# A decoder layer with 32 experts: another list of tasks for the first stage, and earlier loads for the second expert

## The chip, the cores and the metric

The kernel runs on one core of a Trainium2 chip. The metric is the device time of one execution in microseconds; lower is better. A core has TensorE (matmuls, with its weight loads counted apart), VectorE, ScalarE, GpSimd, and the queues that issue transfers: SyncE's (SPq), ScalarE's (ACTq) and GpSimd's (POOLq). All of these share 16 transfer engines. The profile calls the engines PE, PEld, DVE, ACT, POOL and SP.

## The reference

One decoder layer on 512 tokens of width 1024, all in float32. The heart of it:

```python
mod = (silu(c) @ w_ada + b_ada); shift1, scale1, gate1, shift2, scale2, gate2 = split(mod, 6)
h = rmsnorm(x, norm1_w) * (1 + scale1) + shift1
proj = h @ w_in                      # DeltaNet q, k, v, z, a, b and attention q, k, v
o_dn = gated_delta_rule(conv_silu(q), conv_silu(k), conv_silu(v))   # 4 heads of 128, chunks of 64
o_sw = sliding_window_attention(q, k, v, sinks)                     # 8 heads of 64, 2 key heads, window 128
x = x + gate1 * (concat(o_dn, o_sw) @ w_out)
h = rmsnorm(x, norm2_w) * (1 + scale2) + shift2
top_val, top_idx = top_k(h @ w_router + b_router, 4)                # of 32 experts
x = x + gate2 * sum over chosen experts of gate * (swiglu(h @ w_up[e] + b_up[e]) @ w_down[e] + b_down[e])
```

The weights of an expert are 8 MB (up) and 4 MB (down); all 32 experts are used, so 384 MB are read.

## The kernel before, in words

**First stage.** Everything up to the choice of experts. The input is scaled, modulated and projected; the DeltaNet part is prepared for two pairs of heads (`p` = 0, 1): projections and convolutions (`project`, `conv`), lengths, decays, and the inverse of a triangular matrix per chunk (`inverse`, L976 ff.), whose steps go to and fro between TensorE, ScalarE and VectorE. The attention heads (`swa_*`) run beside it. Then `recur` steps through 8 chunks, one after the other; `output` turns each into a part of `oT`. Then for each of the four tiles of 128 tokens (`i` = 0 to 3): `out_swa` and `out_delta` (the output projection, L1142 and L1161, 32 matmuls a tile), `out_end` (adds it to the input), `second_norm`, `route` (router, top 4, slot numbers, and a table that gives each expert's tokens), `finish` (adds the gated bias of the down projection and stores the tile). `ranks` counts the tokens of each expert and orders the experts by count; its result `eri` (L1524) says which expert has which rank. `places` turns table and ranking into `gi`, the rows to gather (L1537), and into `si` and `sg`, the rows to add to and their gates.

**The order of the first stage** is written out by a small planner, `Flow`, while the program is built. Each task is a generator that yields (engine, price in us, buffers wanted) ahead of each step. The planner keeps a clock per engine, takes among the tasks whose next step can start first (within `SLACK`) the one of the lowest priority number (`PR`), and so fixes the order of instructions on each engine. On the chip the engines keep to this order and wait for one another by semaphores. A price that is off therefore costs no time by itself; it puts an instruction at the wrong place in its queue.

**Second stage.** The experts run in a fixed order of ranks (`ORDER`). For each, GpSimd clears a tile and gathers the tokens (`gather`, L1697 and L1698), TensorE transposes them (`turn`), multiplies with the up weights (`up_pass`, L1760), the swiglu runs on VectorE and ScalarE, and TensorE multiplies with the down weights (`down`, L1797); GpSimd adds the rows into the output (`put`). Weights come in pieces of 1 MB through 16 slots, in the order up of expert 0, down 0, up 1, up 2, down 1, up 3, ...; a piece waits until TensorE has used the one that held its slot. The first in the order is always expert 0, so its 12 pieces are issued (`ahead`) before the choice is known. Which expert is second comes from `eri`: GpSimd copies the number to `second` behind the first gather, and SyncE's queue reads it there (`fetch_up(1)`, L1882). Four slots are free for it then (`LATE`); the fifth piece waits for the first step of `up_pass` of expert 0. `load_bias` puts an expert's `b_up` into one of two buffers, `spread_bias` copies it over the rows.

The projections of `project` are done as three single-pass matmuls on high and low parts (`mm3`, L317); most other matmuls are plain float32.

## Time and profile before

| | us |
|---|---|
| median of 3 runs | 1483.18 (1478.5 to 1484.42) |
| the profiled execution | 1480.72 |
| its span, first to last instruction | 1478.9 |
| mean granted clock of TensorE | 0.974 |
| busy: PE, DVE, POOL, ACT | 1381.5, 563.8, 261.1, 237.8 |

A busy TensorE is not TensorE at its peak: the ends of matmuls are modelled and overlap. The rows further down are copied from the trace. A row of a timeline begins with start and length; `x8` counts instructions in one merged row; the bracket behind it tells how long the engine stood idle before and what released it. A row of waits reads: who waited, for whom, us in total, times, longest. Clock 1.00 is 2.4 GHz, 0.50 is 1.2 GHz.

### The profile page before, as it was taken

Reading aid. Unit: us, or ns where it says so; the run is one execution under the profiler, and the core shown is the slowest. Engines: PE = TensorE matmul, PEld = TensorE weight load, DVE = VectorE, ACT = ScalarE, POOL = GpSimd, SP = SyncE. Lnnn points to the kernel's source line nnn. Section 1 sums busy time; section 2 is a strip of 40 time slices with the busy share of each in tenths; the row PEclk is TensorE's granted clock in tenths of the full one; section 3 lists DMA queues with packets and bytes.
Section 4 is the critical chain, followed back from the end, with each engine's and each line's share of the span. In section 5 each row is a group of like instructions: output and inputs, shape, how many; then the busy total and the mean of one; then the engine's idle time right before and its main releaser. Section 6 shows DMA issues by size and latency. Waiting matters only on the chain. (4 is left out here: it accounts for less than half of the span.)

```text
span 1478.9 us, 22303 instructions
## 1 busy us (share of the span) xinstructions
PE 1381.5 (93%) x8586; PEld 601.3 (41%) x8586; DVE 563.8 (38%) x1247; ACT 237.8 (16%) x542; POOL 261.1 (18%) x216
## 2 busy tenths in 40 slices
PE   4999999999879999979999999999999999999974
PEld 3766666765443333322333333333333333343311
DVE  6965567566853222212221231223321323232310
ACT  4354354442211000000000000000000000010000
POOL 2213133202331111101011101102110112211110
PEclk9999999999969999999999999999999999999976
DMA  9655300256349999999999999999998999999995
GB/s 302 212 200 204 113 29 30 58 214 277 116 152 407 409 387 402 396 391 412 411 412 400 379 419 394 384 409 393 410 367 349 403 348 404 393 418 415 414 415 229
DMA packets 104980, 476.16 MB, mean 322 GB/s; under 512 B 13992, under 2 KB 39556, under 8 KB 55714
## 3 DMA queue, kind: packets, MB, share of 16 engines
q1 hardware_dynamic: 91842, 453.16, 77.4%
q0 software_dynamic: 11952, 18.75, 5.5%
q10 hardware_dynamic: 1072, 2.70, 0.5%
q8 instruction: 75, 1.23, 0.3%
q14 instruction: 39, 0.32, 0.1%
HBM read 464.14 MB, written 17.22 MB: 325 GB/s over the span
## 5 line engine op out<-in xcount | busy, mean ns | idle before, releaser
L1760 PE MATMUL ps_up<-we,xTe 128*64 128x512 f32 (+1 forms) x3040 | 622.2, 607 | 21.2 <-DMA we<-in_w_up_dram 16.8
L1760 PEld LDWEIGHTS ps_up<-we,xTe 128*64 128x64 f32 (+1 forms) x3040 | 188.5, 132 | 394.2 <-issue 336.8
L1797 PE MATMUL ps_dn<-we,aT 128*64 128x512 f32 (+1 forms) x1848 | 316.0, 534 | 19.7 <-DMA we<-in_w_down_dram 10.9
L1797 PEld LDWEIGHTS ps_dn<-we,aT 128*64 128x64 f32 (+1 forms) x1848 | 103.7, 129 | 232.2 <-issue 187.2
L1805 POOL DMA_INDIRECT out_dram<-yv,si x52 | 81.7, 1571 | 649.7 <-DVE yv L1804 464.9
L1712 DVE COPY xTe<-ps_xTe 128x256 f32<-128x256 f32 (+3 forms) x35 | 17.5, 501 | 307.4 <-PE ps_xTe L1711 307.4
L1785 ACT COPY aT<-ps_aT 128x512 f32<-128x512 f32 (+1 forms) x52 | 26.0, 530 | 512.5 <-PE ps_aT L1783 509.1
L1769 DVE TENSOR_TENSOR hu<-ps_up,bb 128x512 f32<-128x512 f32 (+1 forms) x52 | 32.1, 617 | 198.8 <-PE ps_up L1760 198.8
L1804 DVE SCALAR_TENSOR_TENSOR yv<-ps_dn,sg,g2p 128x512 f32<-128x512 f32 x38 | 28.5, 751 | 188.3 <-PE ps_dn L1797 187.4
L1771 ACT ACTIVATE hu<-hu 128x512 f32<-128x512 f32 (+1 forms) x52 | 29.8, 573 | 269.4 <-DVE hu L1770 269.4
L1697 POOL MEMSET xg<- 64x1024 f32 (+3 forms) x35 | 37.2, 1084 | 186.0 <-PE ps_xTe L1711 185.8
L317 PE MATMUL ps_ch<-hhi,wih 128*128 128x512 f32 x128 | 58.5, 457 | 0.0
L317 PE MATMUL ps_ch<-hl,wih 128*128 128x512 f32 x128 | 50.8, 397 | 0.0
L317 PE MATMUL ps_ch<-hhi,wl 128*128 128x512 f32 x128 | 50.5, 395 | 0.0
L1720 DVE STREAM_SHUFFLE bb<-bias 128x1024 f32<-128x1024 f32 (+1 forms) x44 | 48.8, 1137 | 0.1
L1712 ACT COPY xTe<-ps_xTe 128x256 f32<-128x256 f32 (+3 forms) x35 | 15.1, 433 | 163.4 <-PE ps_xTe L1711 163.4
L1698 POOL DMA_INDIRECT xg<-h2d,gi x35 | 35.7, 1021 | 16.1 <-POOL xg L1697 8.1
L1711 PEld LDWEIGHTS ps_xTe<-cst,xg 64*128 64x128 f32 (+3 forms) x280 | 24.1, 142 | 32.3 <-issue 23.1
L1783 PEld LDWEIGHTS ps_aT<-cst,act 128*128 128x128 f32 x180 | 24.3, 208 | 28.6 <-issue 25.7
L1711 PE MATMUL ps_xTe<-cst,xg 64*128 64x64 f32 (+3 forms) x280 | 30.1, 249 | 5.1 <-DMA xg<-h2d,gi 2.2
L317 PEld LDWEIGHTS ps_ch<-hhi,wih 128*128 128x128 f32 x128 | 24.2, 189 | 23.2 <-issue 18.0
L1142 PE MATMUL ps_y<-wos,oS 128*128 128x512 f32 x64 | 33.3, 613 | 0.0
(392 smaller groups left out, 1389.0 us busy)
## 6 DMA issues: line engine op xcount, KB each, us to landing
we<-in_w_up_dram SPq DMA_DIRECT2D x256, 1024.0 KB
we<-in_w_down_dram SPq DMA_DIRECT2D x128, 1024.0 KB
wa<-in_w_ada_dram SPq DMA_DIRECT2D x16, 512.0 KB
wi<-in_w_in_dram SPq DMA_DIRECT2D x8, 1024.0 KB
wl<-in_w_ada_dram SPq DMA_DIRECT2D x12, 512.0 KB
oS<-in_w_ada_dram SPq DMA_DIRECT2D x10, 512.0 KB
LL<-in_w_ada_dram SPq DMA_DIRECT2D x10, 512.0 KB
wt<-in_w_in_dram SPq DMA_DIRECT2D x4, 776.0 KB
```

What stands on the lines that cost most here:

```text
L317: TE.matmul(acc, lhsT=w[a], rhs=x_[b], start=start and q == 0, stop=stop and q == 2)
L1142: TE.matmul(a, lhsT=oS[:, j, P * i:P * i + P], rhs=wo[j][:, 512 * hf:512 * hf + 512], start=(j == 0), stop=(j == 3))
L1697: G.memset(xg[:rows_], 0.0)
L1698: state["gather"] = G.indirect_dma_start(out=xg[:rows_], out_offset=None, in_=h2d, in_offset=bass.IndirectOffsetOnAxis(ap=gidx(g)[:rows_], ...
L1711: TE.transpose(pt[:, k, :rows_], xg[:rows_, 512 * hf + P * k:512 * hf + P * k + P], ident[:rows_, :rows_])
L1712: state["turned", hf] = (S.copy if hf else V.tensor_copy)(xt_[:, 4 * hf:4 * hf + 4, :rows_], pt[:, :, :rows_])
L1720: V.stream_shuffle(bbs[w].rearrange("p h n -> p (h n)"), b[w], [0] * 32)
L1760: TE.matmul(t[w * j:w * j + w], lhsT=lhsT, rhs=rhs, start=(k == 0), stop=(k == KT - 1))
L1769: V.tensor_tensor(g, pg, bbs[w][:, 0], op=OP.add)
L1771: S.activation(sgm, g, AF.Sigmoid, scale=1.702)
L1797: TE.matmul(py[u][w * j:w * j + w, 0:m], lhsT=aT[u][:, kt % nf, w * (kt // nf):w * (kt // nf) + w], rhs=wd[kt][:, m * j:m * j + m], start= ...
L1805: G.indirect_dma_start(out=outv[u[1]], out_offset=bass.IndirectOffsetOnAxis(ap=sidx, axis=0), in_=yv, in_offset=None, compute_op=OP.add, b ...
```

## The change

Four things, of which the first is the largest in lines. (1) The planner: most prices are changed, a change between single-pass and float32 matmuls is charged (`SWITCH`), `SLACK` becomes 0, a following step on the same engine counts as ready sooner, and from the last tile's sum on (`hold`) a step is held back when one of clearly lower number would be ready before it ends. Projections are issued two steps (six matmuls) at a time, the late modulation weights three at a time. Priorities change: `yS`, `fin`, and new ones for the last tile, the ranking and the tables, which become tasks of their own (`tabled`). (2) The second expert: SyncE's queue reads `eri` itself; the clears of the first two gathers go to ScalarE. (3) The target lists `si` and `sg` are made by `targets()`, behind the first gathers. (4) One bias buffer instead of two, loaded behind the up pieces; the list of slots is written in another way.

```diff
-SLACK = 0.1
+SLACK = 0.0
+LATES = {0: 3, 3: 6, 6: 8}
-PR = {"swa": 1, "conv": 5, "cend": 4, "in": 4, "late": 1, "z": 2, "load": 1, "yS": 7, "fin": 3, "rt": 4, "yT": 3, "rec": 1, "oout": 2}
+PR = {"ten": (5, 5, 5, 1.5), "last": 0.5, "rank": 0.7, "norm": 1.5, "swa": 1, "conv": 5, "cend": 4, "in": 4, "late": 1, "z": 2, "load": 1, "yS": 4.5, "fin": 5, "rt": 4, "yT": 3, "rec": 1, "oout": 2}
...
+    SWITCH = {"Pr": 0.37, "P": 0.1}
...
         at = max(t[2], self.free[t[3][0][0]])
+        if t[3][0][0] == "P" and t[3][0] != self.kind:
+            at += self.SWITCH[t[3][0]]
...
+                if self.hold:
+
+                    soon = [c for c in can if c[1][3][0][0] == t[3][0][0] and c[1][0] + 1 <= t[0] and c[0] < at + t[3][1]]
+                    if soon:
+                        at, t = min(soon, key=lambda c: (c[1][0], c[0], c[1][1]))
...
+                if t[3] is not None and isinstance(t[3][0], str) and t[3][0][0] == eng and eng in "VSG":
+                    t[2] = min(t[2], at + cost + 0.04)
...
-        for k in range(KT):
+        for k in range(0, KT, 2):
             yield [("win", c0, k // 4)]
-            yield ("P", 0.66) + (("a",) if k == 0 else ())
+            yield ("Pr", 1.40) + (("a",) if k == 0 else ())
...
-            mm3(a, [w[:, P * j:P * j + P] for w in wins[c0, k // 4][k]], hx[k], k == 0, k == KT - 1)
+            for k_ in (k, k + 1):
+                mm3(a, [w[:, P * j:P * j + P] for w in wins[c0, k // 4][k_]], hx[k_], k_ == 0, k_ == KT - 1)
...
+        flow.hold = i == NT - 1
...
+        flow.add(PR["ten"][i], tabled(i, pay, pte, tag))
+
+    def tabled(i, pay, pte, tag):
...
-            flow.add(PR["rt"] - 0.2 * i, route(i))
+            flow.add(PR["rt"] - 0.2 * i if i < NT - 1 else PR["last"], route(i))
...
-        flow.add(PR["rt"] - 0.1, ranks())
+        flow.add(PR["rank"], ranks())
...
-            G.memset(xg[:rows_], 0.0)
+            if early:
+                S.activation(xg[:rows_], bc(one[:rows_], [rows_, D]), AF.Copy, scale=0.0)
+            else:
+                G.memset(xg[:rows_], 0.0)
...
-        e = nc.sync.value_load(second if q == 1 else eri[0:1, r:r + 1], min_val=0, max_val=NE - 1)
+        e = nc.sync.value_load(eri[0:1, r:r + 1], min_val=0, max_val=NE - 1)
...
-        wu = load_up(ws[0], then, THEN if q > 1 else THEN1)
+        wu = load_up(ws[0], (lambda: load_bias(ORDER[0], NB[ORDER[0]], bias)) if q == 1 else None, THEN)
         if q > 1:
+            load_bias(e, NB[r], bias)
             down_of[q - 1] = load_down(state["dn"])
...
         xs = {0: rows_of(0)}
-
-        behind(G.tensor_copy(second, eri[0:1, ORDER[1]:ORDER[1] + 1]), state["gather"])
         ups = {0: ahead[0], 1: fetch_up(1)}
         xs[1] = rows_of(1)
+        targets()
         xT = {0: turn(xs.pop(0))}
         for d in stores[-2:]:
             behind(d, state["turned", 1])
-        bbs = {0: spread_bias(NB[ORDER[0]], bias[0])}
+        bbs = {0: spread_bias(NB[ORDER[0]], bias)}
+        load_bias(state["e1"], NB[ORDER[1]], bias)
```

`targets()` holds the loop over `pieces` that stood at the end of `places`, with the same matmuls and copies. The new prices of steps with a fixed length: 0.17 + 0.00105 n on VectorE (before 0.09 + 0.001 n), 0.17 + 0.00085 n on ScalarE (0.00073), 0.2 + 0.0022 n on GpSimd (0.002); on TensorE for instance 0.65 for 0.45 in the recurrence, 0.96 for 0.56 in the attention's values.

## Rows read from the trace of the kernel before

**Rows 1.** Stages: stretch and length, busy us of engines, clock, DMA share, GB/s

```profile
80.00:308.00 228.00, 224.39 (x2261) 151.80 (x2260) 139.84 (x279) 103.97 (x226) 59.01 (x43) 0.99 0.33 110
308.00:347.00 39.00, 38.40 (x293) 22.75 (x292) 28.57 (x98) 13.85 (x54) 6.12 (x4) 1.00 0.61 221
347.00:411.00 64.00, 58.11 (x255) 28.24 (x253) 46.85 (x128) 11.16 (x34) 16.18 (x13) 1.00 0.53 207
411.00:436.00 25.00, 16.45 (x120) 11.43 (x120) 18.54 (x60) 3.96 (x16) 10.04 (x12) 0.58 0.26 86
436.00:1460.00 1024.00, 983.19 (x5331) 340.22 (x5331) 268.66 (x542) 72.20 (x140) 147.43 (x122) 0.98 1.01 398
```

**Rows 2.** Waits of SyncE's queue, whole program

```profile
SPq L1654 <- DMA we<-in_w_down_dram: 203.5, 96, 4.6
SPq L1654 <- DMA we<-in_w_up_dram: 195.5, 102, 4.7
...
SPq L1882 <- POOL second L1904: 25.8, 1, 25.8
```

**Rows 3.** Waits of TensorE from 436 us on

```profile
PE ps_up L1760 <- DMA we<-in_w_up_dram: 16.8, 17, 1.9
PE ps_dn L1797 <- DMA we<-in_w_down_dram: 10.9, 13, 2.8
```

**Rows 4.** Timeline of TensorE: a run of three, a run of nine, ends

```profile
239.54 0.48 PE L317 MATMUL ps_ch<-hhi,wih 128*128 128x512 f32 x1
...
240.41 1.15 PE L818 MATMUL ps_XT<-XT,Y 64*64 64x64 f32 x32
...
258.19 0.50 PE L317 MATMUL ps_ch<-hhi,wih 128*128 128x512 f32 x1
...
260.48 1.15 PE L818 MATMUL ps_Y<-X,BT 64*64 64x64 f32 x32
```

**Rows 5.** Line 317, 80 to 308 us: min/median/max ns, first and last start

```profile
L317 PE MATMUL ps_ch<-hhi,wl x128: 387/393/558, 79.7 to 308.2; 128*128 128x512 f32 x128
```

**Rows 6.** Timeline of TensorE: first and last step of the second inverse

```profile
236.09 1.15 PE L818 MATMUL ps_X<-cst,XT 64*64 64x64 f32 x32
...
300.70 2.00 PE L1049 MATMUL ps_w<-XT,Kg 64*128 64x64 f32 x16
```

**Rows 7.** Longest wait of VectorE, 347 to 411 us

```profile
DVE yt L1168 <- PE ps_y L1161: 12.0, 4, 4.1
```

**Rows 8.** Timeline, all engines: an earlier tile's step, the tail, the handover

```profile
401.26 0.23 DVE L1326 TENSOR_SCALAR slots<-rt 128x4 f32<-128x4 f32 x1
...
415.69 0.75 DVE L1235 SCALAR_TENSOR_TENSOR h<-h,rt,gm 128x512 f32<-128x512 f32 x1
...
420.17 1.85 POOL L1697 MEMSET xg<- 128x1024 f32 x2
...
420.78 1.26 DVE L1326 TENSOR_SCALAR slots<-rt 128x4 f32<-128x4 f32 x1
...
424.78 0.23 DVE L1513 TENSOR_SCALAR ex<-ex,ec 128x32 f32<-128x32 f32 x1
...
426.75 0.17 ACT L1524 CAST eri<-ps_er 32x32 int32<-32x32 f32 x1 [6.20 <-PE ps_er L1522]
...
429.13 1.10 POOL L1698 DMA_INDIRECT xg<-h2d,gi  x1 [7.12 <-issue]
...
431.47 3.67 SPq L1654 DMA_DIRECT2D we<-in_w_up_dram  x4
...
435.85 5.09 PE L1760 MATMUL ps_up<-we,xTe 128*64 128x512 f32 x16
...
440.98 2.42 SPq L1654 DMA_DIRECT2D we<-in_w_up_dram  x2
```

**Rows 9.** The first four gathers, 425 to 445 us

```profile
DMA to landing us min/median/max: 4.8/8.9/12.4
```

**Rows 10.** Stages again, from the first weight load to the fifth

```profile
431.50:441.00 9.50, 7.23 (x25) 3.00 (x24) 3.04 (x5) 0.58 (x1) 7.03 (x9) 0.62 0.89 275
```

More of the change, by code (lines that the diff above doesn't have):

```diff
@@ L117 @@
     LAT = {"P": 0.12, "V": 0.2, "S": 0.2, "G": 0.2, "D": 2.5, "N": 0.0}
+    SWITCH = {"Pr": 0.37, "P": 0.1}
     def __init__(self, depth):
         self.depth, self.taken, self.back = depth, defaultdict(int), defaultdict(list)
-        self.free, self.done, self.tasks, self.now = defaultdict(float), {}, [], 0.0
+        self.free, self.done, self.tasks, self.now, self.kind, self.hold = defaultdict(float), {}, [], 0.0, "Pr", False
     def mark(self, *key):
@@ L643, in late @@
         for k in range(KT):
-            yield [("lw", r, k)]
-            yield ("P", 0.5) + (("o",) if k == 0 else ())
+            if k not in LATES:
+                continue
+            ks = range(k, LATES[k])
+            yield [("lw", r, k_) for k_ in ks]
+            yield ("P", 0.05 + 0.34 * len(ks)) + (("o",) if k == 0 else ())
             if pa is None:
                 pa = bank("o", "ps_ada")
-            for j in range(4):
-                TE.matmul(pa[32 * j:32 * j + 32, :256], lhsT=bc(cact[:, k:k + 1], [P, 32]), rhs=lw[r, k][:, 256 * j:256 * j + 256],
-                          start=(k == 0), stop=False)
-            flow.give("lp")
-        yield "P", 0.45
+            for k_ in ks:
+                for j in range(4):
+                    TE.matmul(pa[32 * j:32 * j + 32, :256], lhsT=bc(cact[:, k_:k_ + 1], [P, 32]), rhs=lw[r, k_][:, 256 * j:256 * j + 256],
+                              start=(k_ == 0), stop=False)
+                flow.give("lp")
         for j in range(4):
@@ L1162, in out_delta @@
                           start=(j == 0), stop=(j == 3))
[L1163 removed]
+            flow.add(PR["rt"] - 1 if i < NT - 1 else PR["last"], out_end(i, hf, a))
     def out_end(i, hf, a):
[L1166 removed]
+        yield "V", 2 * tv(T), "cv"
         tmp = wk("cv", "yt", 4)
@@ L1271, in route @@
         h2 = wk("x", "h2", 4, D)
-        flow.add(PR["rt"] - 0.2 * i, second_norm(i, ssb, h2))
+        flow.add(PR["rt"] - 0.2 * i if i < NT - 1 else PR["norm"], second_norm(i, ssb, h2))
         room = yield from rooms()
@@ L1481, in output @@
         flow.mark("oT", n)
-    ex = ce.tile([P, 3, NE], F32, name="ex")
-    kr, perm = (ex[:, q] for q in (0, 1))
+    kr = ce.tile([P, NE], F32, name="kr")
     cnt = const.tile([P, NE], F32, name="cnt")
@@ L1494, in layer_kernel @@
     sg = {w: const.tile([P, n, NE], F32, name=f"sg{w}") for w, n in pieces}
-    permc = ex[:, 1:3].rearrange("p c e -> p (c e)")
+    permc = ohs[:, 0:2].rearrange("p c e -> p (c e)")
+    jrow = const.tile([P, 2, 2], F32, name="jrow")
+    for w in (32, 64):
+        G.tensor_copy(jrow[:, w // 64], C("JROW%d" % w))
     def ranks():
@@ L1538, in places @@
         flow.give("d")
-        for w, n in pieces:
-            yield "P", 0.9, "d"
-            pv = bank("d", "ps_sl")[:, :2 * n * NE].rearrange("p (b c e) -> p b c e", c=2, e=NE)
-            for b in range(n):
-                for j in range(P // w):
-                    TE.matmul(pv[w * j:w * j + w, b].rearrange("p c e -> p (c e)"), lhsT=ten[:, 64 * b:64 * b + w], rhs=permc,
-                              start=True, stop=True)
-            yield "S", 0.2
-            S.copy(sg[w], pv[:, :, 1])
-            yield "V", 0.6
-            for b in range(n):
-                V.tensor_scalar(si[w][:, b], pv[:, b, 0], float(P // w), C("JROW%d" % w, b % 2, b % 2 + 1), op0=OP.mult, op1=OP.add)
-            flow.give("d")
     first.close()
@@ L1608, in layer_kernel, with targets @@
     early.close()
+    def targets():
+        for w, n in pieces:
+            pv = pT_.tile([P, 512], F32, name="ps_sl", tag="t")[:, :2 * n * NE].rearrange("p (b c e) -> p b c e", c=2, e=NE)
+            for b in range(n):
+                for j in range(P // w):
+                    TE.matmul(pv[w * j:w * j + w, b].rearrange("p c e -> p (c e)"), lhsT=ten[:, 64 * b:64 * b + w], rhs=permc,
+                              start=True, stop=True)
+            S.copy(sg[w], pv[:, :, 1])
+            for b in range(n):
+                V.tensor_scalar(si[w][:, b], pv[:, b, 0], float(P // w), jrow[:, w // 64, b % 2:b % 2 + 1], op0=OP.mult, op1=OP.add)
     ringe = ctx.enter_context(tc.tile_pool(name="ringe", bufs=RINGE, reuse_waits="tile"))
@@ L1683, in layer_kernel, with gather @@
     LATE[:RING3] = [(ringo, "v")] * (RING3 - 1) + [(ringy, "vy")]
-    bias = [{w: misc.tile([P, 16 * w], F32, name=f"bias{w}{q}") for w in (32, 64)} for q in range(2)]
-    for b in bias:
-        for t in b.values():
-            G.memset(t, 0.0)
+    bias = {w: misc.tile([P, 16 * w], F32, name=f"bias{w}") for w in (32, 64)}
+    for t in bias.values():
+        G.memset(t, 0.0)
     pU = ctx.enter_context(tc.tile_pool(name="pU", bufs=UBANKS, space=PSUM, reuse_waits="tile"))
     pT_ = ctx.enter_context(tc.tile_pool(name="pT", bufs=2, space=PSUM, reuse_waits="tile"))
-    def gather(n, gidx):
+    def gather(n, gidx, early=False):
         xs = []
@@ L1816, in overflow_list @@
             pay = hup.tile([P, 512], F32, name="pay", tag="hu", bufs=TAGS["hu"])
-            _, sum_ = table(i, SW, pay[:, 0:256], [lambda: hup.tile([P, 512], F32, name="sel", tag="hu", bufs=TAGS["hu"])] * 2)
+            steps = table(i, SW, pay[:, 0:256], [lambda: hup.tile([P, 512], F32, name="sel", tag="hu", bufs=TAGS["hu"])] * 2)
+            while True:
+                try:
+                    next(steps)
+                except StopIteration as end:
+                    _, sum_ = end.value
+                    break
             yield
```

93 lines of the change are left out of this document (46 added, 47 removed).

## The prediction

> **What bounds the kernel now.** I read the stages first, then the queue that issues the weights, then the engines that this queue waits for. The stages [rows 1]: from 436 us to 1460 us the transfer engines are busy for the whole time (share 1.01, 398 GB/s), and before 436 us they are half idle or worse (0.33, 0.61, 0.53, 0.26). So the kernel is a first stage of some 436 us, in which the weights of the experts can't flow, and a stream of about 1024 us, which starts when the first stage lets it. The waits of the issuing queue say the same [rows 2]: nearly 400 us on earlier weight loads, and one wait of 25.8 us on `second`, a copy that GpSimd makes behind the first gather. TensorE waits for weights in the stream too [rows 3], 27.7 us in 30 places, so a stream that starts earlier is also consumed earlier. An edit of the first stage is therefore worth what it moves the start of the stream, nearly one for one to the end; TensorE's own idle time inside the stage is worth nothing by itself.
>
> Inside the first stage I asked which engine is full. From 80 to 308 us TensorE counts 224.4 of 228 us, from 308 to 347 us 38.4 of 39 [rows 1]. From 347 to 411 us it is still at 58.1 of 64, VectorE at 46.9. From 411 to 436 us nobody is full (16.5 and 18.5 of 25): that is a chain of dependent steps, at a granted clock of 0.58.
>
> **The change, part by part.** The sum is made against the profiled execution, 1480.7 us (span 1478.9). The median of the runs shown is 1483.2, so 2.5 us are added at the end.
>
> *Fewer changes of matrix mode (80 to 308 us).* The projections run as single-pass matmuls (L317), everything between them as plain float32. Three of them between two float32 groups take 0.87 us (239.54 to 240.41), nine take 2.29 us (258.19 to 260.48) [rows 4]: three runs of three would take 2.61, so breaking a run costs 0.16 us. There are 128 steps of three [rows 5], and I counted 76 unbroken runs in that stretch. The edit issues six matmuls at a time, so at most 64 runs; and since the list now charges a change, some of these join. I take 47 runs: 29 x 0.16 = 4.6 us. Bounds: 12 fewer runs, 1.9 us; 55 fewer, 8.8 us. TensorE is full here, so shorter work is earlier work, unless the chain of the inverse is late instead (a rival below). The late weights in groups of three and the higher prices of the float32 steps change the order only; the same matmuls and loads are issued, and I cost them at nothing, hidden under the full TensorE, with 2 us either way.
>
> *The recurrence (308 to 347 us).* Its eight chunks follow each other through TensorE and VectorE with output projections between. Prices go from 0.45 to 0.65 us, the order hardly. I take 0, with 3 us either way.
>
> *The stretch 347 to 411 us.* Here VectorE idles four times for the last matmuls of an output projection, 12.0 us in all [rows 7]: the old list thought these would be ready. A list with truer prices, in which float32 projections of the attention heads (`yS`, 7 to 4.5) no longer trail, and tables and finishing (`ten` 5, `fin` 5) come behind, should fill some of this. The work itself stays. I take a third, 4 us; bounds 12 us, and -4 us if the tables, put off, pile up on VectorE, which is already at 73%.
>
> *The tail, 411 us to the gather.* In the old order GpSimd's two clears (420.17) stretch a small VectorE step on the chain from 0.23 to 1.26 us [rows 8]; these clears move to ScalarE, 1.0 us. One of tile 3's norm products (0.75 us) stands ahead of the copy that the router waits for; held back, 0.75 us. Against it the ranking now goes ahead of the last table, whose VectorE work follows 424.78: some 0.9 us that were beside the table. Net 0.9 us, say 1; bounds -2 (ScalarE's clear stands behind its last cast and delays the gather) and +5 (rank, norm and finishing all off the chain and the clock up again).
>
> *Start of the second expert's loads.* Old: ranking converted at 426.75, gather issued at 429.13, `second` copied behind it, first load at 431.47 [rows 8]. New: the queue reads the ranking itself, so even at its old place the loads start some 4.5 us sooner. But only four slots are free then. The fifth load waits for TensorE's first step of the up pass: old start 435.85, fifth load 440.98, 5.1 us later [rows 8]. Until that point the old stream did 0.89 x 9.5 = 8.5 us of transfers [rows 10]. The new one can have done the four loads (4 x 1.05 MB at 398 GB/s, 10.5 us) and three gathers (288 rows of 4 KB, 3.0 us): 13.5 us. The lead is thus worth at most 5 us. I take 3, since the stores of the last tile and the bias load, which the edit puts ahead of the fifth load, also wait for their turn; bounds 0 and 5.
>
> *Its price.* The first gather now meets a full queue. Issued at 429.13 on idle transfer engines it landed in 4.8 us, the shortest of the four; the middle one took 8.9 and the longest 12.4 [rows 9]. Full delay 4.1 us by the median, 7.6 by the longest; I take half of the first, 2 us, since part of the four loads has landed by then. The up pass waits for this gather, and the fifth load for the up pass.
>
> This place is where I weighed a rule. The Trainium skill ("DMA: Bandwidth & Descriptors", section "Queues, rings and completion order") says that each transfer engine takes turns between the queues it has work for, packet by packet. By that the gather would not stand behind the four loads but share with them: 0.52 MB at 398 GB/s are 1.3 us, doubled 2.6, so a delay of 1.3 us instead of 2, and the sum would be 0.7 us better. The rows under load (8.9 and 12.4) speak for more than that.
>
> *Target lists, bias, slots.* The 44 target matmuls move behind the gather's issue. TensorE idles there for the gather anyway, but their seven VectorE steps must release the two banks that the transposes of the rows take: 0.5 us, bounds 0 and 1.5. One bias buffer instead of two: a load of bias can start only when the one before is spread, which happens an expert earlier; hidden by the loads queued ahead of it. The rewritten slot list hands out the slots in the same order. Nothing for both; 2 us if the bias is late once.
>
> Sum: 4.6 + 0 + 4 + 1 = 9.6 us earlier gather; minus 2 and 0.5 for the up pass, 7.1 us; plus 3 of lead: the stream stands 10.1 us earlier. 1480.7 - 10.1 = 1470.6 in the profile, 1473 by the median.
>
> **The rivals.**
>
> *Full order gain (chance 0.17).* The stretch 347 to 411 us gives all 12 us, the modes 8, the tail 4: 24 us, minus 2.5, plus 3, is 24.5: 1459. For it: VectorE is idle 17 of the 64 us there. Against it: TensorE is nearly full too.
>
> *Only the handover gains (0.2).* TensorE's saving is eaten by waits inside the inverse, and the order at the end stays bound by both engines: 0 + 0 + 1 + 1 = 2, minus 2.5, plus 3: 2.5 us, 1481. For it: the inverse of the second head pair runs from 236.09 to the last of its products at 300.70 [rows 6], right up to the recurrence, while the filler ends at 308 [rows 5]: both limits lie close together.
>
> *The gather is caught behind the loads (0.07).* With the longest landing, 7.6 us: 9.6 - 7.6 - 0.5 + 3 = 4.5 us, 1479.
>
> *Slower: coarser steps delay the inverse (0.12).* A projection step now holds TensorE 1.58 us (0.87, and three more at (2.29 - 0.87) / 6 = 0.24) and can't be cut, against 0.87. From the first to the last row of [rows 6] the inverse has 19 steps on TensorE, and each finds projections around it. If each waits the longer step's excess in full, 0.71 us, that is 13.5 us; at three quarters, 10. Then the recurrence begins 10 us later however little TensorE has to do, since no output projection can fill the gap before the heads' values and weights are there. -10 + 1 - 2.5 + 3 = -8.5: 1492. It decides when the added wait per step passes 0.24 us (4.6 / 19). Against it: the new list takes float32 steps first whenever one is ready, so a wait is half a step on average (0.35 us of excess at most), and old runs were often longer than three anyway.
>
> **How the numbers follow.** My forecast, about 10 us faster, holds 0.44 (own range 1465 to 1479). A measurement of this kernel tells 0.5% (7.4 us) from no change, so faster means below 1475.8. That is most of the forecast (0.37) and all of the full gain (0.17): 0.54. Same: the rest of the forecast, the handover alone, the caught gather, and a little of the slower case: 0.34. Slower: 0.12. The range from 1457 to 1489 leaves out the far end of the full gain and about half of the slower case.
>
> **What would show it.** Right: first weight load of the second expert before its first gather, the up pass at 427 to 431 us instead of 435.85, the stretch 80 to 308 us shorter by 3 to 7, VectorE's wait for the output projection below 9 us, transfer share 1.0 without a hole from about 5 us after the up pass. Wrong: a hole in the transfers after the four early loads longer than the lead they won; the recurrence starting at or after 304 us; the gather landing later than 9 us; a stream of other length than 1024 us, which would mean that slots or bias hold the queue.

## The result, and the profile after

The changed kernel takes 1470.91 us (median of 5, 1469.78 to 1472.85) against 1483.18 us: ratio 0.9928 [0.9909, 0.9946]. Its profiled execution took 1470.91 us with a span of 1469.1; the one of before took 1480.72 and 1478.9. So the profiles differ by 9.8 us; the prediction's sum was 10.1, and its time 1473. The total came out as forecast, but its terms didn't, as the trace shows.

Stages of the changed kernel, answering to [rows 1] (stretch, length, busy us of PE, PEld, DVE, ACT, POOL, clock, transfer share, GB/s):

```profile
80.00:308.00 228.00, 226.56 (x2346) 162.12 (x2344) 143.62 (x304) 108.55 (x240) 59.04 (x44) 0.99 0.39 136
308.00:347.00 39.00, 37.03 (x226) 21.48 (x225) 23.40 (x74) 9.34 (x40) 7.41 (x5) 0.87 0.19 58
347.00:411.00 64.00, 56.01 (x292) 30.00 (x290) 54.95 (x170) 14.01 (x45) 11.13 (x10) 0.92 0.56 219
411.00:436.00 25.00, 13.16 (x78) 6.93 (x77) 6.49 (x18) 3.40 (x7) 11.97 (x14) 0.53 0.76 260
436.00:1460.00 1024.00, 977.15 (x5365) 337.71 (x5363) 269.16 (x543) 71.61 (x139) 144.53 (x117) 0.99 1.00 394
```

TensorE has 85 matmuls more behind it at 308 us (2346 for 2261), VectorE is busier from 347 to 411 us (54.95 for 46.85), and the transfer engines move weights in the tail (0.76 for 0.26). Fixed stretches show only that work moved. For where time was won and lost I followed landmarks, each read from the timeline of both kernels:

| landmark, us | before | after | earlier by | the prediction's sum |
|---|---|---|---|---|
| first state step of the recurrence (`ps_s`) | 304.23 | 293.14 | 11.1 | 4.6 |
| last state step | 332.85 | 334.85 | -2.0 | 4.6 |
| last output projection (`ps_y`) | 409.56 | 392.88 | 16.7 | 8.6 |
| rows to gather known (`gi`) | 427.98 | 412.43 | 15.6 | 9.6 |
| first gather issued | 429.13 | 419.29 | 9.8 | 9.6 |
| up pass of expert 0 | 435.85 | 431.06 | 4.8 | 7.1 |
| transposes of expert 2, of expert 8 | 470.99, 648.46 | 461.60, 636.37 | 9.4, 12.1 | 10.1 |
| transposes of expert 31, span | 1408.45, 1478.9 | 1397.64, 1469.1 | 10.8, 9.8 | 10.1 |

The rows behind its first four lines, first of the kernel before, then of the changed one (its `gi` follows further down):

```profile
304.23 0.72 PE L1418 MATMUL ps_s<-vn,Kg 64*128 64x128 f32 x8
...
332.85 0.71 PE L1418 MATMUL ps_s<-vn,Kg 64*128 64x128 f32 x8
...
409.56 1.12 PE L1161 MATMUL ps_y<-wod,oT 128*128 128x512 f32 x2
...
427.98 0.28 DVE L1537 TENSOR_SCALAR gi<-ps_gi,cse 128x64 int32<-128x64 f32 x1 [0.82 <-PE ps_gi L1535]
```

```profile
293.14 0.71 PE L1442 MATMUL ps_s<-vn,Kg 64*128 64x128 f32 x8
...
334.85 0.71 PE L1442 MATMUL ps_s<-vn,Kg 64*128 64x128 f32 x8
...
392.88 2.74 PE L1180 MATMUL ps_y<-wod,oT 128*128 128x512 f32 x6
```

The handover in the changed kernel, timeline of all engines, answering to [rows 8]:

```profile
409.41 10.24 SPq L1684 DMA_DIRECT2D we<-in_w_up_dram  x4
...
412.43 0.28 DVE L1563 TENSOR_SCALAR gi<-ps_gi,cse 128x64 int32<-128x64 f32 x1 [0.78 <-PE ps_gi L1561]
...
415.23 0.26 ACT L1389 CAST fin<-ps_gT 96x128 fp32r<-96x128 f32 x1 [3.73 <-PE ps_gT L1387]
415.39 2.00 ACT L1727 ACTIVATE xg<-one 128x1024 f32<-128x1024 f32 x2
...
416.00 1.29 POOL L1401 TENSOR_TENSOR y<-y,bt 128x512 f32<-128x512 f32 x1
417.58 0.56 POOL L1405 DMA_DIRECT2D out_dram<-y  x1 [0.30 <-POOL y L1401]
...
418.14 0.97 POOL L1729 MEMSET xg<- 96x1024 f32 x1
419.29 1.11 POOL L1730 DMA_INDIRECT xg<-h2d,gi  x1 [0.18 <-issue]
...
429.18 1.94 PE L1743 MATMUL ps_xTe<-cst,xg 128*128 128x128 f32 x8 [11.70 <-DMA xg<-h2d,gi]
...
431.06 5.24 PE L1792 MATMUL ps_up<-we,xTe 128*64 128x512 f32 x16
...
434.81 1.19 SPq L1670 DMA_DIRECT2D bias<-in_b_up_dram  x2
436.34 7.66 SPq L1684 DMA_DIRECT2D we<-in_w_up_dram  x4
```

The rows are known 15.6 us earlier, and 10.8 us of that are gone when the up pass begins. Before, the gather was issued 1.15 us after `gi`. Now it takes 6.9 us: ScalarE's clears wait behind its last cast (415.23), and on GpSimd, ahead of the gather, stand the adds and stores of a tile that the list had put off, and a clear. Then the gather, issued 0.64 us after the third load and together with the fourth (418.65 and 419.31 in a closer view of that queue), takes 9.9 us until TensorE begins on its rows (landing 9.8), where the one of before, the first of [rows 9], landed in 4.8.

What moved in that time, in the changed kernel: first from 420.2 to 424 us, then from 424 to 426 us. A row has a queue, its packets, MB, and share of the 16 engines; q1 carries SyncE's loads, q0 GpSimd's gathers.

```profile
q1 hardware_dynamic: 190, 1.43, 88.8%
q0 software_dynamic: 1, 0.00, 0.0%
```

```profile
q1 hardware_dynamic: 82, 0.57, 67.9%
q0 software_dynamic: 142, 0.23, 32.3%
```

So the gather did not wait for the end of the loads. Its first packet came 4.4 us after its issue, and from 424 us on its packets moved beside theirs.

In the stream the waits of TensorE for weights are as before, 28.5 us for 27.7 [rows 3], but VectorE has a new one, for the load of a bias. First the row of the changed kernel, then that of before, both from 436 us on:

```profile
DVE bb L1752 <- DMA bias<-in_b_up_dram: 211.5, 18, 19.4
```

```profile
DVE bb L1720 <- DMA bias<-in_b_up_dram: 31.3, 7, 21.3
```

### The profile page after: what moved, and what is told of

It is laid out like the page before. It is cut to its first block, busy times and chain, and to the rows that moved or that the text cites. A ratio compares the mean times of both kernels' runs of the same rounds, so it can differ in the third digit from the quotient of the medians.

```text
span 1469.1 us, 22280 instructions
## 1 busy us (share of the span) xinstructions
PE 1367.0 (93%) x8586; PEld 603.4 (41%) x8586; DVE 558.6 (38%) x1247; ACT 239.6 (16%) x544; POOL 255.7 (17%) x213
## 5 line engine op out<-in xcount | busy, mean ns | idle before, releaser
L1829 PE MATMUL ps_dn<-we,aT 128*64 128x512 f32 (+1 forms) x1848 | 316.9, 537 | 16.7 <-DMA we<-in_w_down_dram 8.8
L1836 DVE SCALAR_TENSOR_TENSOR yv<-ps_dn,sg,g2p 128x512 f32<-128x512 f32 x38 | 28.5, 751 | 183.7 <-PE ps_dn L1829 182.8
L332 PE MATMUL ps_ch<-hhi,wih 128*128 128x512 f32 x128 | 54.7, 427 | 0.0
```

Of the source, the lines that this page charges most:

```text
L332: TE.matmul(acc, lhsT=w[a], rhs=x_[b], start=start and q == 0, stop=stop and q == 2)
L1829: TE.matmul(py[u][w * j:w * j + w, 0:m], lhsT=aT[u][:, kt % nf, w * (kt // nf):w * (kt // nf) + w], rhs=wd[kt][:, m * j:m * j + m], start= ...
```

## The experiments

Each kernel was timed beside the kernel before; a ratio is to that kernel on the same chip. "Lead" is how much earlier than in the kernel before TensorE begins the transposes of an expert's rows, in the profiled execution; between experts TensorE's work is the same in all these kernels, so the lead changes only where one of them waits. For the kernels that bear on the stream:

```
expert              0      2      7      8     21     22     31
after             4.8    9.4    9.4   12.1   11.5   10.6   10.8
handover alone  -10.0   -4.5   -4.5   -1.3   -2.0   -5.1   -4.8
loads behind     11.8   16.3   16.3   10.9    8.3    2.6    0.4
late cast         8.7   13.4   13.4   16.8   16.3   12.2   12.5
  + two biases    8.6   13.2   13.2   15.8   15.8   15.2   14.7
gather first     11.9   16.5   16.5   15.8   15.1   13.9   14.1
all three        15.0   19.1   19.1   16.7   16.0   16.1   15.9
```

### The handover alone, with the old list

The kernel before with the second expert, clears, targets, bias and slots of the change; prices, steps and priorities stay old.

```diff
-        e = nc.sync.value_load(second if q == 1 else eri[0:1, r:r + 1], min_val=0, max_val=NE - 1)
+        e = nc.sync.value_load(eri[0:1, r:r + 1], min_val=0, max_val=NE - 1)
...
+        targets()
```

> The old list of tasks with the new handover alone (loads of the second expert from the ranking, clears on ScalarE, target lists behind the gathers, one bias buffer). Theory A (the list gains, the handover gives part of it back): the gather is issued later and lands under load in 8 to 10 us, the up pass starts 3 to 6 us later than 435.85, the lead of the loads pays for it; 1478 to 1484 us, no difference from before beyond 0.3%. Theory B (the early loads are the gain): 1472 to 1475 us, two thirds of the change or more.

1483.26 us, ratio 1.0016 [0.9999, 1.0033]: no gain. The loads began at 431.63, the gather was issued at 434.12 and took 9.7 us, the up pass began 10 us later than before. 4.8 us came back between experts 1 and 2: in the kernel before the first bias load stood behind six weight loads, VectorE waited 21.3 us for it, and TensorE for VectorE. Theory A had it. Timeline of the kernel before:

```profile
443.87 6.90 SPq L1640 DMA_DIRECT2D bias<-in_b_up_dram  x4
...
457.10 0.01 DVE L1720 LOAD_MASK_SELECT bb<-bias  x1 [21.30 <-DMA bias<-in_b_up_dram]
...
458.77 7.07 PE L1760 MATMUL ps_up<-we,xTe 128*64 128x512 f32 x24 [2.37 <-DVE xTe L1712]
```

In the changed kernel this bias lands at 437.55, since it is issued ahead of the fifth load. In the table every kernel with this handover gains 4.1 to 5.5 us between experts 0 and 2.

### The second expert's loads behind the gather again

```diff
-        e = nc.sync.value_load(eri[0:1, r:r + 1], min_val=0, max_val=NE - 1)
+        e = nc.sync.value_load(second if q == 1 else eri[0:1, r:r + 1], min_val=0, max_val=NE - 1)
...
+        behind(G.tensor_copy(second, eri[0:1, ORDER[1]:ORDER[1] + 1]), state["gather"])
```

> The changed kernel, but the second expert's number is read again from a copy that GpSimd makes behind the first gather. Theory A: the gather meets idle transfer engines and lands in about 5 us instead of 9.9, the up pass starts near 426 instead of 431 us, the first load of the second expert near 421.5 instead of 409.4; the lost lead and the earlier up pass cancel: 1468 to 1474 us. Theory B: the lead is lost and nothing comes back: 1478 to 1482 us.

1481.72 us, ratio 1.0007 [0.9993, 1.002]. The gather met idle transfer engines and TensorE began on its rows 4.2 us after the issue; the up pass came at 424.1, 7 us earlier than in the changed kernel. And yet the whole gain of the change is gone. The table shows where: 5.4 us between experts 7 and 8, where TensorE waits for weights whose loads began at 420.33 for 409.41, and 5.7 us between 21 and 22, where VectorE's wait for a bias ends so late that TensorE idles and its clock falls (0.66 over 10 us). Stage and timeline of this kernel there:

```profile
1075.00:1085.00 10.00, 6.45 (x20) 2.33 (x20) 2.34 (x4) 0.48 (x1) 2.97 (x3) 0.66 1.02 385
```

```profile
1076.76 0.01 DVE L1752 LOAD_MASK_SELECT bb<-bias  x1 [13.02 <-DMA bias<-in_b_up_dram]
...
1078.69 0.90 PE L1743 MATMUL ps_xTe<-cst,xg 96*128 96x96 f32 x4 [3.55 <-DVE xTe L1744]
```

So the early loads are worth 10.8 us in the medians with the new list. Theory B had the time, theory A the up pass. But 5.7 us of the 10.8 were lost by way of the single bias buffer; what would be left of them with two buffers was not tested. Neither half of the change gains alone: not the handover (1.0016), and not the list with the loads behind the gather.

### Single projection steps and no mode price

```diff
-    SWITCH = {"Pr": 0.37, "P": 0.1}
+    SWITCH = {"Pr": 0.0, "P": 0.0}
...
-        for k in range(0, KT, 2):
+        for k in range(KT):
             yield [("win", c0, k // 4)]
-            yield ("Pr", 1.40) + (("a",) if k == 0 else ())
+            yield ("Pr", 0.88) + (("a",) if k == 0 else ())
...
-            for k_ in (k, k + 1):
+            for k_ in (k,):
```

> The changed kernel, but projections issued three matmuls at a time (price 0.88 us) and changes of matrix mode not charged. Theory A: 65 to 76 unbroken runs instead of 38, the recurrence starts 6 to 8 us later (299 to 301 instead of 293 us); the recurrence had given that back anyway, so the time moves by less than 4 us: 1470 to 1475. Rival: TensorE is the bound of the whole first stage, and the time goes up by the full 6 to 8 us: 1477 to 1479.

1500.38 us, ratio 1.0139 [1.0116, 1.0163], far slower than either theory allowed. The projections lie in 64 unbroken runs (38 in the changed kernel, 76 before), the recurrence starts at 318.6, and TensorE idles 12.5 us up to 310 us (1.3 in the changed kernel). Both parts at once didn't tell which it was, so the next took one.

### Paired steps, no mode price

```diff
-    SWITCH = {"Pr": 0.37, "P": 0.1}
+    SWITCH = {"Pr": 0.0, "P": 0.0}
```

> The changed kernel with its paired projection steps at 1.40 but the price of a change of mode at 0. By the written order TensorE then changes to the projections and back 54 times in place of 38. In the changed kernel the projections end at 288.25 (308.2 before), the recurrence starts at 293.1 and the up pass at 431.06. With single steps at 0.88 and no mode price, 64 changes, the recurrence began at 318.6 and TensorE was idle 12.5 us before it (2.2 in the changed kernel). Theory A (each change costs 0.16 us, as my prediction had it): 16 more changes are 2.6 us, recurrence at 295 to 297, time 1472 to 1475. Theory B (what counts is that the list then misjudges TensorE's time and lets the inverse's steps wait, whatever the number of changes): idle time above 6 us, recurrence after 300, time 1477 or more.

1485.55 us, ratio 1.0022 [1.0008, 1.0035]: theory B. (The changed kernel's idle time, 2.2 us in the expectation, is 1.3 us in the trace.) With this number left out, the rest of the change gains nothing. 54 runs instead of 38, but TensorE's time from one projection matmul to the next instruction adds up to 98.0 us instead of 96.6, so the changes themselves cost 1.4 us. The recurrence starts 16.5 us later for other reasons: 7.0 us of idle time instead of 1.3 (up to the recurrence), half clock behind it, and 3.7 us more of output projections done ahead. Stages of this kernel, then of the changed one:

```profile
216.00:224.00 8.00, 3.68 (x31) 2.63 (x32) 6.12 (x13) 3.09 (x8) 5.71 (x5) 0.90 0.13 18
224.00:232.00 8.00, 8.00 (x37) 5.04 (x38) 3.85 (x9) 2.24 (x4) 1.91 (x2) 0.50 0.52 115
```

```profile
216.00:224.00 8.00, 7.10 (x113) 5.18 (x114) 7.59 (x10) 5.24 (x12) 4.94 (x4) 1.00 0.39 120
224.00:232.00 8.00, 8.00 (x118) 5.96 (x117) 5.58 (x14) 4.67 (x14) 3.52 (x3) 1.00 0.05 16
```

A list that thinks TensorE sooner free than it is puts steps ahead whose inputs aren't there.

### New prices, old priorities

```diff
-PR = {"ten": (5, 5, 5, 1.5), "last": 0.5, "rank": 0.7, "norm": 1.5, ..., "yS": 4.5, "fin": 5, ...}
+PR = {"ten": (3.4, 3.4, 3.4, 3.4), "last": 3, "rank": 3.9, "norm": 3.4, ..., "yS": 7, "fin": 3, ...}
```

> The changed kernel with the new prices and the paired projection steps, but the priorities of the kernel before. In the changed kernel the state recurrence begins 11.1 us earlier than before (293.1 for 304.2) and takes 13 us longer, since 25 matmul groups of the output projection (36.9 us) run between its start and its end, 17 (19.7 us) before; the last output projection is 16.7 us earlier. Theory A (prices and steps give the first 11 us; the priorities only move output projections into the recurrence, which costs there what it saves later): recurrence starts at 293 to 296, is 28 to 32 us long, last output projection at 397 to 401, places known at 415 to 420, time 1473 to 1477. Theory B (the priorities make the early start too, the longer runs of projections come from them): recurrence starts after 300, last output projection after 404, time 1479 to 1483.

1473.6 us, ratio 0.9947 [0.9933, 0.9962]. The time is theory A's, but half of its reason falls: with the old priorities the recurrence is as long, 292.8 to 334.4, with 34 matmuls of output projections between its first and last state step (34 in the changed kernel, 20 before). So both the early start and the filled recurrence come from what the new list has besides its priorities. The priorities give the last output projection 4.0 us (396.8) and `gi` 5.5 (417.9); the longer way from `gi` to the gather in the changed kernel (6.9 us for 3.5) takes most of that back, and 2.7 us are left in the medians, whose intervals overlap. The first gather of this kernel was issued ahead of the third load, and yet landed only after 10.1 us:

```profile
421.39 1.11 POOL L1730 DMA_INDIRECT xg<-h2d,gi  x1 [0.34 <-ACT xg L1727]
...
421.79 0.99 SPq L1684 DMA_DIRECT2D we<-in_w_up_dram  x2
```

### Output projections kept out of the recurrence

```diff
-        yield [("wos",), ("y1", i), ("values", i, 1), ("g1",)]
+        yield [("wos",), ("y1", i), ("values", i, 1), ("g1",), ("oT", 4 + i) if i else ("oT", 3)]
```

> The changed kernel with each output projection of the window attention made to wait for a late chunk of the recurrence (tile 0 for chunk 3, tiles 1, 2, 3 for chunks 5, 6, 7). In the changed kernel 25 groups of output projections, 36.9 us, lie between the recurrence's start (293.1) and its last output chunk (348.3), and its state steps take 41.7 us (28.6 before). By the written order 4 of the single projection matmul groups then stand before the last state step in place of about 19. Theory A (the two places are worth the same: TensorE is full in both): state steps 28 to 32 us long, last output projection within 4 us of 392.9, time 1469 to 1474. Theory B (the filled recurrence is a gain of its own, since later the projections wait for VectorE's product and add): recurrence as short, but the last output projection after 402, time 1478 to 1482. Theory C (the long recurrence is a loss that the change should have avoided): last output projection before 388, time below 1467.

1479.27 us, ratio 0.9975 [0.9961, 0.9989], in the main theory B: the state steps take 30.8 us instead of 41.7 with 6 such matmuls between them, but the last output projection begins at 400.1, 7.2 us later, and `gi` is known at 420.0, 7.6 later. So filling the recurrence, which looked like a loss of 13 us in the landmarks, is a gain. Later, each projected tile has VectorE's sums and the router behind it: from 325 to 436 us TensorE waits 6.0 us for VectorE's `h` and `bt`, and in the changed kernel it has no such waits. That this makes up the 7 us is argued, not tested.

### No hold

```diff
-        flow.hold = i == NT - 1
+        flow.hold = False
```

> The changed kernel without the rule that holds back a late step once the last output tile is closed (hold stays False); prices, priorities and steps as in the change. Only the order behind the last out_end moves. In the changed kernel the last output projection began at 392.88, the places were known at 412.43 (19.6 us later; 18.4 in the kernel before), and the up pass began at 431.06. Theory A (in this tail the steps hang on one another and the clock is at half speed; the order of what is ready changes little): places within 1.5 us of 412.4, time 1469 to 1472. Theory B (the hold is what keeps the tail from growing, since more late steps now wait there): places 3 to 6 us later, time 1473 to 1476.

1475.82 us, ratio 0.9945 [0.9929, 0.9961]; its profiled execution took 1473.0, so 2 to 5 us against the changed kernel, in intervals that overlap. `gi` comes 3.2 us later, as theory B has it. GpSimd's adds now lie beside VectorE's selections: two of these take 1.65 us, while four took 1.13 us alone. The two pairs lose 2.2 us by it; that these are part of the 3.2 us is read from the rows, not tested. Timeline of this kernel, then of the changed one:

```profile
398.55 1.65 DVE L1213 TENSOR_SCALAR room<-cst,slots 128x256 f32<-128x256 f32 x2
398.79 1.25 POOL L1401 TENSOR_TENSOR y<-y,bt 128x512 f32<-128x512 f32 x1 [9.34 <-DVE bt L1397]
...
400.72 1.65 DVE L1213 TENSOR_SCALAR room<-cst,slots 128x256 f32<-128x256 f32 x2
400.95 1.26 POOL L1401 TENSOR_TENSOR y<-y,bt 128x512 f32<-128x512 f32 x1
```

```profile
394.30 1.13 DVE L1213 TENSOR_SCALAR room<-cst,slots 128x256 f32<-128x256 f32 x4
```

### The cast of the down bias behind the recurrence

In the changed kernel TensorE's two state steps at 310 and 322 us lie 11.8 us apart. ScalarE's queue stands there at a cast whose load is late, and while GpSimd's subtraction behind it runs, a VectorE step of the recurrence takes 2.17 us instead of 0.28. Timeline of the changed kernel:

```profile
312.68 1.04 ACT L1145 CAST bdh<-bdx 96x1024 fp32r<-96x1024 f32 x1 [2.83 <-DMA bdx<-in_b_down_dram]
313.85 2.33 POOL L1147 TENSOR_TENSOR bdh<-bdx,bdh 32x1024 fp32r<-32x1024 f32 x1 [4.30 <-ACT ssd L1491]
314.10 2.17 DVE L1495 TENSOR_SCALAR on<-on,ssd 128x128 f32<-128x128 f32 x1 [1.87 <-ACT ssd L1492]
316.40 3.62 PE L1236 MATMUL ps_sb<-fix,s2c 128*128 128x32 f32 x16 [1.97 <-DVE s2c L1231]
```

```diff
         state["bdr"] = bdr = bdh.bitcast(F32R)
+        yield [("oT", 7)]
```

> The changed kernel, but the high and low parts of the down projection's bias (a cast on ScalarE that waits for its load, and a subtraction of 2.33 us on GpSimd) wait for the end of the recurrence. In the changed kernel one VectorE step of the recurrence takes 2.17 us instead of 0.28 beside that subtraction, TensorE idles 1.97 us and then runs at half the clock until 325 us. Theory A: this stall goes, the recurrence takes 36 to 38 us instead of 42 and the time falls by 3 to 5 us: 1466 to 1468. Rival: the stretch behind it is bound by VectorE and takes the gain away: 1470 to 1472, the recurrence shorter all the same.

1468.49 us, ratio 0.9911 [0.989, 0.9931]. The last state step is 3.4 us earlier than in the changed kernel, of which 1.2 us were there at the first one, and the up pass 4.0. The medians lie 2.4 us apart with intervals that overlap, so the landmarks and not the time show this gain. The recurrence takes 39.5 us instead of 41.7, still far from the 28.6 of before: the same two state steps lie 9.5 us apart. The router's bias (`ps_sb`) still stands between them, and the clock falls here too, although TensorE is counted busy throughout. Stages of this kernel:

```profile
308.00:314.00 6.00, 6.00 (x53) 4.11 (x52) 3.17 (x14) 1.07 (x5) 1.11 (x1) 1.00 0.43 91
314.20:320.80 6.60, 6.60 (x28) 4.87 (x28) 1.51 (x7) 1.11 (x6) 0.00 (x0) 0.50 0.00 0
```

So idle time alone doesn't account for the half clock of the changed kernel there (0.50 from 315 to 325 us); what does stays open. In the table the lead is larger by 4 to 5 us up to expert 21 and by 1.7 at the end: the rest went mostly between experts 21 and 22, where TensorE waited 1.92 us for VectorE at 1069.13.

### Late cast and two bias buffers

```diff
-    bias = {w: misc.tile([P, 16 * w], F32, name=f"bias{w}") for w in (32, 64)}
+    bias = [{w: misc.tile([P, 16 * w], F32, name=f"bias{w}{q}") for w in (32, 64)} for q in range(2)]
...
-        if q > 1:
-            load_bias(e, NB[r], bias)
+        wu = load_up(ws[0], ... if q == 1 else lambda: load_bias(e, NB[r], bias[q % 2]), THEN if q == 1 else 2)
```

> The changed kernel with the cast of the down bias behind the last state step (as in the run before with that alone, 1468.5) and, new, two bias tiles in turn as in the kernel before, the bias load among the up loads of its expert again. In the changed kernel VectorE waits for a bias load 18 times in the expert stage, 211 us in all (before: 7 times, 31 us); one of these ends so late, at 1071.8, that TensorE waits 1.74 us for VectorE's copy of a turned tile at 1073.7, and with the late cast the wait at 1069.1 is 1.92 us and the clock falls (0.78 over 1060 to 1075): there the lead over the kernel before shrinks from 16.3 to 12.2 us. Theory A (the single bias tile is what costs that): VectorE's wait for the bias falls below 50 us, no such wait at 1070, the lead stays near 16 us to the end, and the time is 1464 to 1465.5. Theory B (the lead is lost there because the weights or the buffers of the ring limit the next experts whatever VectorE does): TensorE waits as long for weights at 1080 to 1240, and the time stays at 1468 to 1469.

1467.26 us, ratio 0.9901 [0.9884, 0.9918]. VectorE's wait for the bias falls from 199.6 us with the late cast alone to 10.2, TensorE no longer waits for VectorE at 1070, and the loss between experts 21 and 22 falls from 4.1 to 0.6 us. The mechanism is theory A's, the size is not: at the end 2.3 us in the lead, and 1.2 us in the medians, whose intervals overlap. VectorE's waits of this kernel from 436 us on:

```profile
DVE bb L1754 <- DMA bias<-in_b_up_dram: 10.2, 5, 2.9
```

### Nothing ahead of the first gather

The finishing of the third tile on VectorE and ScalarE's queue instead of GpSimd, the last cast on VectorE, and the third clear on ScalarE.

```diff
-            (G if i < NT - 1 else V).tensor_tensor(yv, yv, tmp, op=OP.add)
+            (G if i < NT - 2 else V).tensor_tensor(yv, yv, tmp, op=OP.add)
...
-            stores.append((G if i < NT - 1 else S).dma_start(
+            stores.append((G if i < NT - 2 else S).dma_start(
...
-        S.copy(gT, pg[:3 * NE, 0:P])
+        (S.copy if i < NT - 1 else V.tensor_copy)(gT, pg[:3 * NE, 0:P])
...
-        return gather(NB[r], lambda g: gi[:, g, r:r + 1], q < 2)
+        return gather(NB[r], lambda g: gi[:, g, r:r + 1], q < 3)
```

> The changed kernel, with what stood ahead of the first gather taken out of its way: the finishing adds of the third token tile go to VectorE and its stores to ScalarE's queue (both were GpSimd's), the last cast of gT goes to VectorE, and the gathers' third tile is cleared by ScalarE too. In the changed kernel the places were known at 412.43, the gather was issued at 419.29 and landed at 429.15, the up pass began at 431.06, the fifth load of the second expert at 436.34. Theory A (the 6.9 us between the places and the gather are a new wait of the change, and the stream of weights, which starts anew when the up pass frees buffers, comes earlier with it): gather issued near 414, up pass at 423 to 425, fifth load at 429 to 431, and time 5 to 6 us below the changed kernel's: 1465 to 1466. Theory B (the weights that have landed decide where TensorE next waits, at 613 to 650 us, and what the gather gains is spent there): the up pass begins 6 to 8 us earlier all the same, TensorE's waits for weights between 600 and 650 grow by as much, and the time stays at 1469 to 1471.

1471.17 us, ratio 0.9931 [0.9916, 0.9945]: in the medians no gain over the changed kernel; the profiled execution, 1467.54 us, is the fastest of its six. The gather came at 417.62 only, held by ScalarE's clears, yet the up pass at 423.96: issued 1.25 us ahead of the third load, it landed in 4.3 us. Timeline of this kernel:

```profile
417.62 1.10 POOL L1730 DMA_INDIRECT xg<-h2d,gi  x1 [5.65 <-ACT xg L1727]
...
418.87 0.99 SPq L1684 DMA_DIRECT2D we<-in_w_up_dram  x2
...
422.09 1.94 PE L1743 MATMUL ps_xTe<-cst,xg 128*128 128x128 f32 x8 [5.21 <-DMA xg<-h2d,gi]
```

The lead of 7.1 us over the changed kernel at expert 7 is 3.7 at expert 8: the weights decide there, as theory B says, though TensorE's waits for them grew little. Between the two theories, and unsettled in time.

### All three edits

The three diffs above together.

> All three edits on the changed kernel: late cast of the down bias, nothing ahead of the first gather, two bias tiles. Theory A (each lead goes through to the end once VectorE doesn't wait for the bias): up pass at 419 to 421, time 1459 to 1462. Theory B (the weights' arrival between 600 and 650 takes back what the gather gains, as when the loads were put behind the gather): 1464 to 1467, with TensorE's waits for weights between 600 and 650 above 10 us (7.2 in the changed kernel counted over the same lines).

1463.88 us, ratio 0.9879 [0.9861, 0.9898]: the fastest kernel of this study, 7 us below the changed one. Theory B's numbers: the up pass began at 420.8, and TensorE's waits for weights from 600 to 650 us were 10.7 us. Kernels whose up pass began at 427.1 (late cast), 424.0 (gather first) and 420.8 (all three) all stand 15.8 to 16.8 us ahead at expert 8. These three and the late cast with two biases also moved 370 GB/s alike from 400 to 613 us (361 in the changed kernel), which speaks for the weights as the limit; what sets their rate stays open. From 436 us on the stream moved fewer bytes per us in the last of them than in the first, at much the same share of the transfer engines (stages: all three edits first, the late cast alone second):

```profile
436.00:600.00 164.00, 163.28 (x860) 57.67 (x855) 45.76 (x81) 13.88 (x25) 23.71 (x20) 1.00 1.02 393
```

```profile
436.00:600.00 164.00, 162.83 (x860) 57.86 (x858) 44.95 (x80) 13.48 (x24) 22.71 (x19) 1.00 1.01 401
```

## Why the prediction came out, term by term

That the sum fits so well is luck: its terms were off by +6.0 us up to the rows known (15.6 for 9.6), -8.3 from there to the up pass (-10.8 for -2.5), and +3.0 in the lead (6.0 for 3), which nearly cancel. What held is the direction: the list gives the start, the handover takes part of it back, and the lead grows in the stream.

- **Fewer changes of mode: 4.6 us predicted, 11.1 earlier at that landmark.** The price was right, the count of saved changes low: of 76 unbroken runs 38 were left, where I took 47. Adding up TensorE's time from each projection matmul to the next start gives 100.9 us for the 375 that came ahead of the recurrence before, and 96.6 for all 384 now: 4.3 us, or 6.7 at an equal number, 0.18 us for each of 38 changes (0.16 predicted). What I had costed at nothing gave the rest: the late weights in groups of three 2.8 us, less idle time 2.3, smaller groups 1.7. That the right mode price also keeps steps from standing too early is the larger effect, 14.6 us in the medians of the kernel without it, and was nowhere in my sum.
- **The recurrence: 0 predicted, 13 lost.** It had been filled to 308 us by projections, which are now done. In TensorE's time from first to last state step the output projections took 8.5 us more (34 matmuls in 18.3 us for 20 in 9.8), the router's bias, which stood behind the last state step before, 5.3, and idle time 1.4; the projections took 2.5 less. Half clock, for 10.2 us of it, is in these numbers. A late cast stalled it too, but moving the cast gave back only 2.2 us of the length.
- **The stretch after it: 4 predicted, 18.7 measured.** VectorE's waits for output projections [rows 7] fell from 12.0 to 2.7 us there, so this source held, but most is the work that had moved into the recurrence. The two terms belong together: 5.6 us, where I had 4. Keeping the projections out of the recurrence made the kernel slower by 8 us.
- **The tail: 1 predicted, -1.1 measured** (from the last output projection to `gi` 19.6 us for 18.4). The clock stays near half speed there (0.53 from 411 to 436 us, 0.58 before). The kernel without the hold is 2 to 5 us slower, where I had put 0.75, though the intervals overlap.
- **From the places to the up pass: -2.5 predicted, -10.8 measured.** This step failed. I had only given a clear on ScalarE that "stands behind its last cast and delays the gather" as a bound of 2 us; it and GpSimd's put-off finishing took 5.7. The gather under load took 5.0 us more, not 2. Both my 2 us and the 1.3 us weighed beside them left out that its first packet comes late: 4.4 us after the issue, and 1.7 us in the four kernels whose gather landed early. The order of issue doesn't decide it alone: the landing took 4.3 us when the gather was issued 1.25 us ahead of the third load, 9.8 us when 0.64 us behind it, but 10.1 us with the old priorities, 0.40 us ahead. In all 13 kernels a gather was early (4.1 to 4.8 us) where GpSimd's issuing instruction, of some 1.1 us, had ended before the third load of the second expert was issued, and late (9.2 to 10.6 us) where it had not; no run tests this by itself, and why the packets come late stays open. The Trainium skill ("DMA: Bandwidth & Descriptors", section "Queues, rings and completion order") says that a transfer engine takes turns between its queues packet by packet. The rows from 424 to 426 us, in which both queues move, agree with it; of the 4.4 us before the first packet it tells nothing.
- **The lead of the stream: 3 predicted, 6.0 measured** (4.8 at the up pass to 10.8 at expert 31). 4.6 us of it come between experts 0 and 2, by the first bias load ahead of the fifth weight load, which I had counted as a delay only. 2.7 come around expert 8, where the kernel before runs short of weights; only these are what the term was meant for. The single bias buffer, which I had costed at nothing and bounded by 2 us, then takes 0.9.

The rivals: the handover alone brings nothing, the full order gain didn't come, and steps of six matmuls did not delay the inverse (the last matmul of its product `ps_w` begins at 291.7 instead of 302.4 us). The gather was caught behind the loads, by 5.0 us of the 7.6 of that rival, but the rows were known 6 us earlier than in its sum. Of the signs of being wrong that I had named, two came: the gather landed later than 9 us, and from the up pass to the end the changed kernel takes 1038.0 us instead of 1043.1. The transfers have a hole too (share 0.40 from 430 to 436 us, 0.78 from 436 to 443).

My first premise, that a move of the stream's start is worth its length to the end, is refuted by the kernel with the loads behind the gather. Its up pass came 11.8 us earlier than before and the second expert's first load 11.1, but of that lead 0.4 us were left at expert 31: the rest went on the way, at waits for weights and for a bias.

## What to carry to other kernels

In a list of tasks with prices, the price that nobody charges (here a change of matrix mode) did harm by putting steps where their inputs weren't ready, far beyond its own length (14.6 us against 1.4); charge it before tuning priorities. When a chain is shortened, look for what the planner had put off to the place where the chain now ends: it stands ahead of the handover on the same queues. And follow the gain expert by expert; a lead can be lost hundreds of microseconds later at a wait that was harmless while everything was late.

## What the runs showed of the hardware that was not expected

A gather that meets 1 MB loads of another queue can land some 5 us late (9.2 to 10.6 us for 4.1 to 4.8), even when its issue began 0.40 us ahead of one of them. In these kernels it was early only where the issuing instruction, of some 1.1 us, had ended before the third load was issued.

A GpSimd operation can hold up a VectorE step until it ends: a step of 0.28 us took 2.17 us, to 316.27 us, beside a subtraction of 2.33 us that had started 0.25 us before and ended at 316.18. The Trainium skill ("SBUF — State Buffer", section "SBUF: two separate sides") says that the two engines share a pair of ports as an exclusive lock: between a GpSimd operation and certain kinds of VectorE operation, the one that starts first holds it for its whole instruction. The two ends agree with that; whether this step is of such a kind, no run shows.

In the kernel without the mode price 4.3 us of idle TensorE between 216 and 224 us were followed by 8 us at half clock (0.50, 224 to 232 us), so a stall was paid nearly twice. With the late cast the clock fell to 0.50 from 314.2 to 320.8 us with TensorE counted busy throughout.
